# Seven modulation vectors on TensorE at the stage changes, the others on VectorE

## The chip, the cores and the metric

The kernel runs on one core of one Trainium2 chip. The metric is the device time of one execution in microseconds (us); the time before is the median of three runs. Everything shown of one execution comes from the hardware profiler. Engines are called PE (TensorE matmul), PEld (its weight load), DVE (VectorE), ACT (ScalarE), POOL (GpSimd) and SP (SyncE, which issues the transfers).

## The reference

Two networks follow one another on 256 tokens of width 1024, each two layers deep. Every layer is modulated: a vector of 6 x 1024 numbers is a product of the conditioning vector `c` and a 1024 x 6144 matrix, and its six parts shift, scale and gate the two halves of the layer.

```python
c_act = jax.nn.silu(c)
for l in range(DEPTH):
    mod = c_act @ ada_w[l] + ada_b[l]
    sh1, sc1, g1 = mod[:, None, 0:D], mod[:, None, D:2 * D], mod[:, None, 2 * D:3 * D]
    sh2, sc2, g2 = mod[:, None, 3 * D:4 * D], mod[:, None, 4 * D:5 * D], mod[:, None, 5 * D:6 * D]
    h = rmsnorm(x, norm1_g[l]) * (1.0 + sc1) + sh1
    x = x + g1 * token_mix(h, ...)
    h = rmsnorm(x, norm2_g[l]) * (1.0 + sc2) + sh2
    x = x + g2 * grouped_moe(h, ...)
```

The second network has the same frame with a gated linear recurrence (layer 0), a chunked attention (layer 1) and a 4096-wide MLP in each layer. With two more vectors for its shared keys and values there are 26 modulation vectors of 1024, numbered v = 0 to 25; `v = 6 * layer + part` with the four layers in order.

## The kernel before

The activations `xT` stay in SBUF, transposed, as 8 tiles of 128 x 256. All weights come from HBM once, as pieces of 128 x 2048 numbers (1 MB). A piece goes through a ring of 5 buffers (`raw`), is cut into a high and a low part (`parts_of`: ACT casts at L442, DVE subtracts at L443), and each product takes three matmuls of these parts (`mm3`, L453 to L455).

The stages follow one another: token mix, router and experts (MoE) for each layer of the first network, then recurrence, MLP, attention, MLP. Between two of them PE has to wait. The sum of squares of the new `xT` (`stats_add`) goes through DVE and POOL (`stats_close`, `power`), PE spreads it over the partitions (`rstd_x`, tile `ps_bc`), and `norm_mod` makes the next input `h_hi`, `h_lo` tile by tile on DVE and ACT. After the token mix it is the router (`route`) that PE waits for, twice: for the one-hot groups `oh` ahead of the matmuls into `ps_sl`, and for the gather matrix `both` ahead of `ps_xg`. At the end of each MoE stands a branch (`tc.If(big > 0)`, L1487) that every engine takes.

A modulation vector is 4 units of 1 MB. `ada_unit` computes a unit in one of two ways. On PE it is 8 matmuls into `adaps` (L331), 32 columns wide, four of them side by side; each shows as two records. The fourth unit is copied by ACT and folded by two further matmuls (`ada_flush`, tile `ps_mod`, L347). On DVE, for the vectors in the table `ON_DVE`, it is two fused multiply-and-sum instructions over 128 x 1024 (`ada_dve`, L305).

The units stand in one list (`pend`, L684). At numbered places of the program (`ada_site`, L364) the table `FILL` says how many units are taken from it, one where the table is silent. The program is written once; a scheduler then orders the instructions of every engine, and it may put matmuls of one unit between those of other work. `issue_after` holds an instruction behind a given one.

Of the kernel before, what the change touches and what calls it, by code (L numbers as in the profile page):

```python
# [53 lines left out]
ON_DVE = (2, 5, 6, 7, 8, 9, 12, 13, 14, 15, 19, 20, 24, 25)  # L54
# [128 lines left out]
def program(tc, A, out, dbg=None):  # L183
    nc = tc.nc
    from contextlib import ExitStack, nullcontext
    with ExitStack() as st:
# [129 lines left out]

        def ada_unit(u):
# [4 lines left out]
            raw = ring.tile([P, RING], F32, tag="raw", name="raw")  # L322
            nc.sync.dma_start(raw, A["ada"][u])
# [126 lines left out]

        def mm3(ps, a, b, start, stop):
# [1424 lines left out]
```

## Time and profile before

| | us |
|---|---|
| median of 3 runs (1825.03 to 1833.75) | 1825.52 |
| the profiled execution, its own time | 1829.82 |
| its span, first to last instruction | 1828.0 |

| engine | busy us | share of the span | instructions |
|---|---|---|---|
| PE | 1748.5 | 96% | 12430 |
| PEld | 1548.3 | 85% | 12430 |
| DVE | 1465.6 | 80% | 2514 |
| ACT | 1130.7 | 62% | 1758 |
| POOL | 37.4 | 2% | 40 |

Busy means that an instruction of the engine was in execution. Matmuls overlap and their ends are modelled, so a busy PE isn't PE at its peak. The transfers moved 485.62 MB, a mean of 266 GB/s. In the rows further down, times count from the start of the span, "x" is a count of records, PEclk is the granted TensorE clock (1.00 is 2.4 GHz, 0.50 is 1.2 GHz), and the square brackets at the end of a timeline row hold how long the engine had been idle and who released it.

### The profile page before, as it was taken

To read this page: it belongs to the slowest core of one execution; us is meant where nothing else is said; L and a number is where in the kernel's file an instruction comes from. 1 tells how busy PE (TensorE), PEld (TensorE's weight loads), DVE (VectorE), ACT (ScalarE), POOL (GpSimd) and SP (SyncE) were. 2 spreads that over 40 slices of the span, in tenths; PEclk is the share of its full clock that TensorE was granted. 3 is DMA by queue.
4 is the path that set the end of the run, shared out by engine and by line. 5 is a ranking of instruction groups with operands and counts; after the bars stand their busy time and mean duration, and the time that the engine had idled before them with its cause. 6 is when DMAs were issued, how large, how long until landed. Compare 5 with 4: busy or idle time off the path is not lost. (4 is left out here: it accounts for less than half of the span.)

```text
span 1828.0 us, 31671 instructions
## 1 busy us (share of the span) xinstructions
PE 1748.5 (96%) x12430; PEld 1548.3 (85%) x12430; DVE 1465.6 (80%) x2514; ACT 1130.7 (62%) x1758; POOL 37.4 (2%) x40
## 2 busy tenths in 40 slices
PE   7999998999999899998999999899999999999999
PEld 5877897888877897887888887798899988889999
DVE  4878897999998676888998999788898666667754
ACT  4754546877777556545877777578655446546642
POOL 0000000000000000000000000000000002100000
PEclk9999999999999899998999999899999999999999
DMA  9665797797998357688697899656687764456552
GB/s 354 234 248 213 278 358 278 287 348 278 350 346 343 137 191 265 233 323 343 253 343 301 328 354 354 236 202 251 221 322 284 272 250 146 173 191 256 204 193 84
DMA packets 71727, 485.62 MB, mean 266 GB/s; under 512 B 8720, under 2 KB 10896, under 8 KB 14352
## 3 DMA queue, kind: packets, MB, share of 16 engines
q1 hardware_dynamic: 70992, 483.21, 70.7%
q8 instruction: 101, 1.65, 0.4%
q14 instruction: 58, 0.48, 0.1%
q10 hardware_dynamic: 576, 0.27, 0.1%
HBM read 482.41 MB, written 1.05 MB: 264 GB/s over the span
## 5 line engine op out<-in xcount | busy, mean ns | idle before, releaser
L443 DVE TENSOR_TENSOR wlo<-raw,whi 128x1024 fp32r<-128x1024 f32 (+1 forms) x628 | 753.0, 1210 | 152.2 <-ACT whi L442 135.8
L442 ACT CAST whi<-raw 128x1024 fp32r<-128x1024 f32 (+1 forms) x628 | 649.7, 1041 | 282.8 <-PE ps_mm L454 164.6
L453 PE MATMUL ps_mm<-h_hi,whi 128*128 128x256 f32 x1168 | 329.7, 285 | 5.5 <-ACT h_hi L649 3.5
L454 PE MATMUL ps_mm<-h_lo,whi 128*128 128x256 f32 x1168 | 327.9, 282 | 0.7 <-DVE h_lo L650 0.7
L455 PE MATMUL ps_mm<-h_hi,wlo 128*128 128x256 f32 x1168 | 327.4, 282 | 1.0 <-DVE wlo L443 1.0
L453 PEld LDWEIGHTS ps_mm<-h_hi,whi 128*128 128x128 f32 x1168 | 222.0, 191 | 11.9 <-ACT h_hi L649 5.3
L454 PEld LDWEIGHTS ps_mm<-h_lo,whi 128*128 128x128 f32 x1168 | 222.6, 191 | 2.6 <-DVE h_lo L650 0.9
L455 PEld LDWEIGHTS ps_mm<-h_hi,wlo 128*128 128x128 f32 x1168 | 221.6, 190 | 3.6 <-DVE wlo L443 2.7
L454 PE MATMUL ps_e<-wlo,xg 128*128 128x512 f32 x512 | 202.5, 396 | 2.6 <-DVE wlo L443 2.3
L453 PE MATMUL ps_e<-whi,xg 128*128 128x512 f32 x512 | 202.7, 396 | 1.2 <-ACT whi L442 1.0
L455 PE MATMUL ps_e<-whi,xg 128*128 128x512 f32 x512 | 200.3, 391 | 0.0
L455 PE MATMUL ps_mm<-a_hi,wlo 128*128 128x256 f32 x512 | 142.2, 278 | 0.2 <-DVE wlo L443 0.2
L454 PE MATMUL ps_mm<-a_lo,whi 128*128 128x256 f32 x512 | 142.3, 278 | 0.0
L453 PE MATMUL ps_mm<-a_hi,whi 128*128 128x256 f32 x512 | 142.2, 278 | 0.0
L305 DVE SCALAR_TENSOR_TENSOR raw<-raw,cb 128x1024 f32<-128x1024 f32 x112 | 135.7, 1217 | 3.5 <-DMA raw<-in_ada_dram 3.4
L454 PEld LDWEIGHTS ps_e<-wlo,xg 128*128 128x128 f32 x512 | 96.2, 188 | 27.2 <-DVE wlo L443 8.5
L453 PEld LDWEIGHTS ps_e<-whi,xg 128*128 128x128 f32 x512 | 96.2, 188 | 20.9 <-ACT whi L442 1.8
L455 PEld LDWEIGHTS ps_e<-whi,xg 128*128 128x128 f32 x512 | 96.1, 188 | 18.5
L454 PE MATMUL py<-wlo,hT 128*128 128x512 f32 x256 | 101.0, 394 | 0.0
L455 PE MATMUL py<-whi,hT 128*128 128x512 f32 x256 | 99.8, 390 | 0.0
L453 PE MATMUL py<-whi,hT 128*128 128x512 f32 x256 | 99.5, 391 | 0.0
L455 PEld LDWEIGHTS ps_mm<-a_hi,wlo 128*128 128x128 f32 x512 | 96.0, 187 | 0.4 <-DVE wlo L443 0.4
(694 smaller groups left out, 3471.4 us busy)
## 6 DMA issues: line engine op xcount, KB each, us to landing
raw<-in_ada_dram SPq DMA_DIRECT2D x104, 1024.0 KB, 6.1
raw<-in_mw_dram SPq DMA_DIRECT2D x64, 1024.0 KB, 4.9
raw<-in_w_up_dram SPq DMA_DIRECT2D x56, 1024.0 KB, 5.0
raw<-in_w_down_dram SPq DMA_DIRECT2D x56, 1024.0 KB, 5.0
raw<-in_w_gate_dram SPq DMA_DIRECT2D x44, 1024.0 KB, 4.9
raw<-in_win_dram SPq DMA_DIRECT2D x34, 1024.0 KB, 5.2
more<-in_w_gate_dram SPq DMA_DIRECT2D x12, 1024.0 KB, 5.4
raw<-in_lwin_dram SPq DMA_DIRECT2D x11, 1024.0 KB, 7.4
```

Source lines behind the costliest of these rows:

```text
L305: nc.vector.scalar_tensor_tensor(w, w, 1.0, cb, op0=OP.mult, op1=OP.mult, accum_out=mod[:, m:m + 1])
L442: nc.scalar.copy(hi[:, :n], src)
L443: nc.vector.tensor_sub(lo[:, :n], src, hi[:, :n].bitcast(F32))
L453: nc.tensor.matmul(ps, ah, bh, start=start, stop=False)
L454: nc.tensor.matmul(ps, ah, bl, start=False, stop=False)
L455: nc.tensor.matmul(ps, al, bh, start=False, stop=stop)
```

## The change

Before, 12 vectors are computed on PE (0, 1, 3, 4, 10, 11, 16, 17, 18, 21, 22, 23) and 14 on DVE. After it, 9 are on PE and 17 on DVE. Of the nine, vectors 1 and 0 stay where they are, in the first 50 us. The other seven (5, 8, 11, 14, 17, 20, 23: the gates) leave the list and get places in the seven stage changes: `GAPS` says how many of the four units stand ahead of the last sum of squares or the router's sums, how many after it, and how many behind `ps_bc` (or behind `ps_sl`). `in_turn` ties the matmuls around them into that order, and their folding waits for the next `ada_flush`. At the end of a MoE their four loads are issued early (`EARLY_U`), and of the next stage's weights one piece is fetched ahead instead of three. `FILL` is new, and its default is no unit. In the core of the diff:

```diff
-ON_DVE = (2, 5, 6, 7, 8, 9, 12, 13, 14, 15, 19, 20, 24, 25)
+ON_DVE = (2, 3, 4, 6, 7, 9, 10, 12, 13, 15, 16, 18, 19, 21, 22, 24, 25)
+GAPS = {5: (0, 3, 1), 8: (0, 2, 2), 11: (0, 3, 1), 14: (0, 3, 1), 17: (1, 1, 2), 20: (1, 1, 2), 23: (1, 1, 2)}
...
+        def in_turn():
+            return tc.issue_after(PE_[0].ins) if PE_[0] else nullcontext()
+
+        def ada_load(u):
+            if u in EARLY_U:
+                return EARLY_U.pop(u)
+            raw = ring.tile([P, RING], F32, tag="raw", name="raw")
+            nc.sync.dma_start(raw, A["ada"][u])
+            return raw
...
-            ada_flush()
+            if u // 4 not in GAPS:
+                ada_flush()
...
+        def gap(v, i):
+            u = 4 * v + sum(GAPS[v][:i])
+            with in_turn():
+                for j in range(GAPS[v][i]):
+                    ada_unit(u + j)
...
-            ada_fill(FILL.get(i, n))
+            ada_fill(FILL.get(i, 0))
...
-        def stats_close(rt=None):
+        def stats_close(rt=None, v=None):
+            if v:
+                PE_[:] = LAST
+                gap(v, 0)
+                with in_turn():
+                    stats_late()
             stats_late()
...
-            for i in range(n):
-                nc.tensor.transpose(ps[:, i * P:(i + 1) * P], ST["rt"][:, i:i + 1].to_broadcast([P, P]), ident)
+            for i in (2, 3, 0, 1)[4 - n:]:
+                with in_turn():
+                    PE_[:] = [nc.tensor.transpose(ps[:, i * P:(i + 1) * P], ST["rt"][:, i:i + 1].to_broadcast([P, P]), ident)]
...
-        def norm_mod(a_col, b_col, rs=None, fill=0):
+        def norm_mod(a_col, b_col, rs=None, v=0):
             if rs is None:
                 rs = rstd_x()
-            ada_site(fill)
+            ada_site(0)
+            gap(v, 2)
...
-        pend += [4, 5, 6, 7, 0, 1, 2, 3] + list(range(8, 84)) + list(range(96, 104)) + list(range(84, 96))
+        pend += [4, 5, 6, 7, 0, 1, 2, 3] + [4 * v + i for v in ON_DVE[:-4] + (24, 25, 21, 22) for i in range(4)]
...
                 ada_site(TURN_1)
+                gap(5 + 6 * l, 1)
...
-                nc.tensor.matmul(pp[:, 0:4], lowb, oh[:, 0, :], start=True, stop=True)
+                with in_turn():
+                    nc.tensor.matmul(pp[:, 0:4], lowb, oh[:, 0, :], start=True, stop=True)
...
+                gap(5 + 6 * l, 2)
...
                             ready(nxt[:1])
+                            for u in range(32 + 24 * l, 36 + 24 * l):
+                                EARLY_U[u] = ada_load(u)
...
-                prefetch(nxt[1:])
+                prefetch(nxt[1:2])
+                gap(8 + 6 * l, 1)
+                PE_[0] = None
```

Line numbers of the changed kernel are 10 to 40 higher for the same code: L342 is its L331, L303 its L305.

**PE, router of layer 0.** `lowb` and `oneb` are constant matrices, `ps_ht` is the transposed input, `ps_sl` counts the tokens of each group. Before:

```order
L1212 MATMUL ps_ht<-c_ident,y 128x128
L583 MATMUL ps_ms<-c_wr,y 128x16
L1212 MATMUL ps_ht<-c_ident,y 128x128
L1254 LDWEIGHTS lowb
L1254 MATMUL ps_sl<-oh,lowb 128x4
L1255 LDWEIGHTS oneb
```

And now:

```order
L1241 MATMUL ps_ht<-c_ident,y 128x128
L605 MATMUL ps_ms<-c_wr,y 128x16
L1241 MATMUL ps_ht<-c_ident,y 128x128
L342 MATMUL adaps<-raw,crep 32x256 x24
L1285 LDWEIGHTS lowb
L1285 MATMUL ps_sl<-oh,lowb 128x4
L1286 LDWEIGHTS oneb
```

Three units of vector 5 have come between the last transposition and the group counts; the fourth stands behind the counts. Layer 1 has the same with vector 11.

**PE, end of the MoE of layer 0**, behind the branch (the row of `ps_ms` belongs to the path that isn't taken). Before:

```order
L583 MATMUL ps_ms<-one,sq 128x1 x2
L1487 UNCONDITIONAL_BRANCH x2
L632 MATMUL ps_bc<-c_ident,rx 128x128 x2
L453 MATMUL ps_mm<-h_hi,whi 128x256 x2
L454 MATMUL ps_mm<-h_lo,whi 128x256
L455 MATMUL ps_mm<-h_hi,wlo 128x256
```

And now:

```order
L605 MATMUL ps_ms<-one,sq 128x1 x2
L1524 UNCONDITIONAL_BRANCH x2
L342 MATMUL adaps<-raw,crep 32x256 x15
L660 MATMUL ps_bc<-c_ident,rx 128x128 x2
L342 MATMUL adaps<-raw,crep 32x256 x8
L475 MATMUL ps_mm<-h_hi,whi 128x256 x2
L476 MATMUL ps_mm<-h_lo,whi 128x256
L342 MATMUL adaps<-raw,crep 32x256 x8
L477 MATMUL ps_mm<-h_hi,wlo 128x256
```

One matmul of vector 8 stands ahead of the branch and 15 stand behind it, ahead of `ps_bc`. At the end of layer 1 it is 5 matmuls of vector 14 ahead of the branch and 19 behind it.

**DVE, heads of the token mix of layer 1** (`at` is the attention matrix of a head, `mk` its masked part). Before:

```order
L443 TENSOR_TENSOR wlo<-raw,whi 128x384
L972 TENSOR_TENSOR at_7832<-at_7832,mk 128x2x64
L972 TENSOR_TENSOR at_7832<-at_7832,mk 128x4x32
L972 TENSOR_TENSOR at_7832<-at_7832,mk 128x8x16
L972 TENSOR_TENSOR at_7832<-at_7832,mk 128x16x8
L972 TENSOR_TENSOR at_7832<-at_7832,mk 128x32x4
L972 TENSOR_TENSOR at_7832<-at_7832,mk 128x64x2
```

And now:

```order
L463 TENSOR_TENSOR wlo<-raw,whi 128x1024
L1001 TENSOR_TENSOR at_7837<-at_7837,mk 128x2x64
L303 SCALAR_TENSOR_TENSOR raw,mod<-raw,cb 128x1024
L1001 TENSOR_TENSOR at_7837<-at_7837,mk 128x4x32
L1039 TENSOR_TENSOR rt<-ps_rot,sn 128x256
L1001 TENSOR_TENSOR at_7837<-at_7837,mk 128x8x16
L1040 TENSOR_TENSOR qt<-qt,cs 128x256
```

Modulation instructions have come between a head's own. Between the scale `qsc` and the first output `ob_lo` of the other attention there are now 11 where there was none (layer 0: 9 where there were 4). The count of these instructions goes from 38 to 48 in the token mix of layer 1 and from 34 to 48 from the first MLP on; in layer 0 it stays 40.

## Rows read from the trace of the kernel before

**Rows 1.** Table by stretch, all work: length, PE, PEld, DVE, ACT, POOL busy, PEclk.
```profile
106.00:163.00 57.00, 54.73 (x422) 40.89 (x422) 43.49 (x165) 30.70 (x74) 4.36 (x5) 1.00 0.58 218
679.00:733.00 54.00, 53.13 (x442) 42.15 (x442) 38.70 (x123) 32.85 (x75) 3.29 (x4) 1.00 0.63 234
1166.00:1277.00 111.00, 107.41 (x933) 97.25 (x934) 93.34 (x173) 79.06 (x138) 0.00 (x0) 0.97 0.62 230
1317.00:1493.00 176.00, 175.26 (x1488) 174.05 (x1487) 136.87 (x210) 88.46 (x134) 0.00 (x0) 1.00 0.77 281
1518.00:1623.00 105.00, 101.84 (x866) 85.68 (x864) 69.59 (x181) 62.15 (x161) 14.07 (x13) 1.00 0.45 166
```

**Rows 2.** The same for tile `adaps` alone: length, PE, PEld, ACT busy, PEclk.
```profile
106.00:163.00 57.00, 13.27 (x128) 4.00 (x128) 0.74 (x2) 1.00 0.58 218
679.00:733.00 54.00, 10.82 (x128) 3.50 (x128) 0.75 (x2) 1.00 0.63 234
1166.00:1277.00 111.00, 13.60 (x160) 5.03 (x160) 0.73 (x2) 0.97 0.62 230
1518.00:1623.00 105.00, 10.13 (x112) 3.55 (x112) 0.38 (x1) 1.00 0.45 166
```

**Rows 3.** Groups of instructions: shapes, count, busy us, mean ns, idle before.
```profile
L305 DVE SCALAR_TENSOR_TENSOR raw<-raw,cb 128x1024 f32<-128x1024 f32 x112 | 135.7, 1217 | 3.5 <-DMA raw<-in_ada_dram 3.4
```

**Rows 4.** The chain that ended last, by line, 1166 to 1277 and 1518 to 1599.
```profile
by line: PE ps_mm L453 11.6%; PE ps_mm L454 10.8%; PE ps_mm L455 10.1%; DVE wlo L443 9.2%; PE adaps L331 7.9%; issue 6.8%; ACT whi L442 6.7%; DMA raw<-in_lwin_dram 5.3%; DMA raw<-in_band_dram 2.9%; ACT r L1616 2.6%; ACT r L1629 2.0%; ACT s_
by line: PE ps_mt L453 11.1%; PE ps_mt L454 9.7%; PE ps_mt L455 9.6%; PE ps_mm L453 9.2%; PE ps_mm L454 9.1%; PE ps_mm L455 8.0%; PE ps_ao L1180 5.5%; PE adaps L331 4.5%; PE ps_sc L1795 4.4%; POOL rk L549 3.9%; PE ps_pt L1172 3.1%; PE ps_hn
```

**Rows 5.** Timeline: a run of modulation records, at 2.4 and at 1.2 GHz.
```profile
1647.56 1.93 PE L331 MATMUL adaps<-raw,crep 128*32 128x256 f32 x30
1167.39 1.93 PE L331 MATMUL adaps<-raw,crep 128*32 128x256 f32 x16
```

**Rows 6.** Timeline of PE at the router of layer 0.
```profile
288.80 0.16 PE L1254 MATMUL ps_sl<-oh,lowb 128*128 128x4 bf16 x1 [3.38 <-DVE oh L1241]
291.01 0.55 PE L1316 MATMUL ps_xg<-both,ht_hi 128*128 128x256 f32 x1 [1.94 <-DVE both L1266]
```

**Rows 7.** The branch: its line on PE's queue (ns), then PE behind it.
```profile
L1487 PEldq COMPARE_BRANCH  x2: 3843/4712/5582, 594.3 to 1158.5; - x2
...
598.58 0.66 PE L632 MATMUL ps_bc<-c_ident,rx 128*128 128x128 f32 x2 [3.08 <-DVE gh L1130]
600.41 0.80 PE L453 MATMUL ps_mm<-h_hi,whi 128*128 128x256 f32 x2 [1.18 <-ACT h_hi L649]
...
1164.62 1.09 PE L632 MATMUL ps_bc<-c_ident,rx 128*128 128x128 f32 x4 [4.44 <-PEq L1487]
```

**Rows 8.** Timeline of PE: first product of the first MLP and of the attention.
```profile
1308.65 1.22 PE L453 MATMUL ps_mm<-h_hi,whi 128*128 128x256 f32 x4 [1.11 <-ACT h_hi L649]
1498.60 0.58 PE L453 MATMUL ps_mt<-whi,h_hi 128*128 128x256 f32 x1 [1.52 <-ACT h_hi L649]
```

**Rows 9.** Table by stretch at stage changes; after POOL: PEclk, DMA share, GB/s.
```profile
245.00:299.00 54.00, 45.98 (x373) 44.26 (x372) 46.51 (x101) 27.44 (x47) 0.70 (x1) 0.94 0.88 351
287.70:294.50 6.80, 3.76 (x21) 3.71 (x21) 5.96 (x17) 2.95 (x6) 0.00 (x0) 0.50 1.01 428
847.50:857.70 10.20, 5.03 (x29) 4.70 (x29) 7.64 (x24) 5.01 (x9) 0.70 (x1) 0.50 1.01 426
591.50:605.20 13.70, 9.45 (x41) 8.80 (x42) 7.06 (x19) 4.19 (x10) 0.70 (x1) 0.50 0.17 69
1154.70:1171.80 17.10, 11.34 (x57) 9.08 (x57) 8.87 (x25) 6.51 (x13) 1.01 (x1) 0.50 0.31 109
1308.30:1311.70 3.40, 3.05 (x14) 3.05 (x15) 3.40 (x10) 2.35 (x6) 0.00 (x0) 0.50 0.50 207
1496.00:1502.90 6.90, 4.99 (x22) 4.59 (x23) 5.38 (x14) 2.98 (x7) 0.34 (x1) 0.51 1.01 427
1643.00:1655.00 12.00, 11.54 (x125) 8.72 (x125) 8.87 (x22) 6.12 (x12) 0.70 (x1) 1.00 0.84 343
```

More of the change, by code (lines that the diff above doesn't have):

```diff
@@ L315, in ada_step @@
                 tiles.pop(0)()
+        EARLY_U = {}
+        PE_ = [None]
+        def in_turn():
[6 more added lines that the diff above has]
+            return raw
         def ada_unit(u):
@@ L321, in ada_unit @@
                 return ada_dve(u)
-            raw = ring.tile([P, RING], F32, tag="raw", name="raw")
-            nc.sync.dma_start(raw, A["ada"][u])
+            raw = ada_load(u)
             i, ps = 0 if u < 48 else 1, adaps[:, u // 4 % 2]
@@ L449, in parts_of @@
             return w
+        LAST = [None]
         def mm3(ps, a, b, start, stop):
@@ L673, in stats_late, with last_linear @@
                 stats_add(LATE_M.pop())
-        def last_linear(pcs, kt, x, gcol, fill=0, also=None):
+        def last_linear(pcs, kt, x, gcol, fill=0, also=None, v=None):
             stats_open(also=also)
             linear(pcs, kt, x, residual(gcol, True), fill)
-            stats_close()
-        pend += [4, 5, 6, 7, 0, 1, 2, 3] + list(range(8, 84)) + list(range(96, 104)) + list(range(84, 96))
+            stats_close(v=v)
+        pend += [4, 5, 6, 7, 0, 1, 2, 3] + [4 * v + i for v in ON_DVE[:-4] + (24, 25, 21, 22) for i in range(4)]
         with ExitStack() as es:
@@ L879, in token_mix @@
                     ada_site(HM)
-                    h = norm_mod(gain(at[f"n1_{l}"], M(0, l, 1)), M(0, l, 0), fill=NM)
+                    h = norm_mod(gain(at[f"n1_{l}"], M(0, l, 1)), M(0, l, 0), v=8)
                     linear(pc(0, 512), 8, h, ev_f, 0, True)
@@ L1299, in moe @@
                 ada_site(TURN_2)
-                ada_flush()
                 ready([(A["w_gate"][l * NE * 2], 0, 4, 0, 512)])
@@ L1376, in moe @@
                 back(0, 2)
+                ada_flush()
+                if two:
+                    c_columns(1)
                 U = {}
@@ L1501, in moe @@
                     stats_all(two, rt)
+                PE_[0] = None
         LAM = {}
@@ L1562, in recurrent @@
                 nc.vector.tensor_mul(ga, ga, at["fin"])
-                h = norm_mod(ga, M(1, 0, 0), rs=rs[:, T:], fill=NL)
+                h = norm_mod(ga, M(1, 0, 0), rs=rs[:, T:], v=14)
                 xc = (lr.tile([P, 11, T], F32R, name="xc_hi"), lr.tile([P, 11, T], F32R, name="xc_lo"))
@@ L1692, in recurrent @@
                         residual(M(1, 0, 2), True)(c + i, accs[c + i])
-                stats_close()
+                stats_close(v=17)
         def mlp(l):
@@ L1702, in mlp @@
                 ada_site((HP, HQ)[l])
-                h = norm_mod(gain(at[f"m2_{l}"], M(1, l, 4)), M(1, l, 3), fill=(NP, NQ)[l])
+                gap(17 + 6 * l, 1)
+                h = norm_mod(gain(at[f"m2_{l}"], M(1, l, 4)), M(1, l, 3), v=17 + 6 * l)
                 a = (mp.tile([P, 32, T], F32R, name="a_hi"), mp.tile([P, 32, T], F32R, name="a_lo"))
@@ L1715, in mlp @@
                 if l + 1 < DEPTH:
-                    last_linear(*out_, M(1, l, 5), FM)
+                    last_linear(*out_, M(1, l, 5), FM, v=20)
                 else:
@@ L1732, in chunk_attn @@
                 ada_site(HA)
+                gap(20, 1)
                 rs = ap_.tile([P, T], F32, name="rs")
                 nc.scalar.copy(rs, rstd_x())
-                hk = norm_mod(gain(at["kvn"], mod[:, o + 8:o + 16]), mod[:, o:o + 8], rs=rs, fill=NA)
+                hk = norm_mod(gain(at["kvn"], mod[:, o + 8:o + 16]), mod[:, o:o + 8], rs=rs, v=20)
                 h = (ap_.tile([P, 8, T], F32R, name="hq_hi"), ap_.tile([P, 8, T], F32R, name="hq_lo"))
@@ L1842, in chunk_attn @@
                 linear(wo[1:], 8, oo, out_, FA)
-                stats_close()
+                stats_close(v=23)
         for l in range(DEPTH):
```

18 lines of the change are left out of this document (9 added, 9 removed), and 10 rows, old and new, of the table FILL.

## The prediction

> **What bounds the kernel now.** I read the table by stretch first. PE is busy for 54.73 of 57 us in the heads of layer 0, for 53.13 of 54 in those of layer 1, for 107.41 of 111 in the recurrence and for 175.26 of 176 in the first MLP, always ahead of DVE [rows 1]. So PE sets the pace inside the stages. The same table for the tile `adaps` alone says how much of that is modulation: 13.27, 10.82, 13.60 and 10.13 us in four stretches, 47.82 us in all, made by 528 records, that is 33 of the 48 units [rows 2]. This is what could leave PE's path. But DVE is not far behind in the same stretches: 43.49 of 57, 38.70 of 54, 93.34 of 111, 69.59 of 105 [rows 1], and the price of a vector on DVE is high: 8 instructions of 1217 ns [rows 3], 9.7 us, three vectors more are 29 us. So the question in each stretch is how far it can shrink before DVE ends it.
>
> **The change, part by part.** The sum is made against the profiled execution, 1829.8 us; the median of the runs lies 4.3 lower, at 1825.5.
>
> *Heads of layer 0.* PE loses 13.27 us. DVE gets 5 modulation instructions more between the same two landmarks, 5 x 1.217 = 6.1, so 43.49 + 6.1 = 49.6 us of DVE in a stretch of 57: it can't shrink by more than 7.4 us, and by nothing if the heads' own chain sets it. I take 6, near the upper end, since PE stood still for only 57 - 54.73 = 2.3 us.
>
> *Heads of layer 1.* PE loses 10.82 us, DVE gets 11 more, 13.4 us: 38.70 + 13.4 = 52.1 of 54. At most 1.9 us; I take 1.5.
>
> *Recurrence.* PE loses 13.60 us and DVE gets nothing here. The chain that ended last says what of it was on the path: 7.9% of 111 us, 8.8 us [rows 4]. The same row has 5.3%, 5.9 us, for the landing of a recurrence weight; its piece shares the five ring buffers with modulation loads that are now gone, and I take 2 of them. Together 10.8; the ends are 8.8 and 13.6 + 5.9 = 19.5.
>
> *Attention.* PE loses 10.13 us. In the first 81 us of the stretch the chain has 4.5%, 3.6 us, for it [rows 4]; the last 24 us have no such row, and of what lies there, 10.13 less what the first part holds, about 4.9, I take half: 6.0. Ends 3.6 and 10.1.
>
> Sum of what goes: 24.3 us, between 12 and 39.
>
> *What comes into the waits.* The price of a unit: 30 records, 15 matmuls, took 1.93 us at 2.4 GHz and 16 records the same at 1.2 GHz [rows 5], so a unit of 8 matmuls is 1.03 or 1.93 us.
>
> At the router PE waits 3.38 us for `oh` and 1.94 us for `both` [rows 6]. Three units (3.1 us) and one (1.0) fit in. Cost 0, in both layers; a cover of 0.3 and 0.9 us is left, so it costs something as soon as a load is late.
>
> At the end of the MoE it is different. PE's branch takes 3.84 us in layer 0 and 5.58 in layer 1 on its own queue, and the waits ahead of `ps_bc`, 3.08 and 4.44 us, are this branch [rows 7]: the row that releases it is PE's sequencer, or DVE released by it. The order puts 15 matmuls of vector 8 (19 of vector 14) behind the branch and ahead of `ps_bc`, so they don't fill the wait, they prolong it: 1.93 us (2.4) at full clock, 3.6 (4.6) at half. Queued behind them are `ps_bc`, then DVE's and ACT's chain of `h_hi`, `h_lo`, and all of the next stage. The unit after `ps_bc` meets a wait of 1.18 us [rows 7] and overhangs by 0 or 0.75; layer 0 has another unit among the products, 1.03 or 1.93. Ends 3.0 and 6.3 for layer 0, 2.4 and 5.4 for layer 1. The granted clock there is 0.50 from 591.5 to 605.2 and from 1154.7 to 1171.8 [rows 9], so I stay nearer to the upper ends: 5 + 4 = 9. Whoever took the 3.08 and 4.44 us for idle time to be filled would write 0 here, and get 9 us less. The Trainium skill, Runtime: NRT & Kernel Launch, section on instruction fetch mechanics, speaks for the reading above: a taken branch whose target is not in the window already fetched makes the engine fetch the target before it goes on, so by that page no work behind the branch can cover it. The two durations of 3.84 and 5.58 us agree.
>
> Before the two MLPs and the attention, the first unit has the wait for the last squares, the second the wait for POOL, and two units (2.06 us) stand behind `ps_bc`, where PE waits 1.11 and 1.52 us [rows 8]: overhang 0.95 + 0.5, I take 1.5, and 0 where the tiles of `h` come slowly enough to take it up. The change from attention to the second MLP has its four units there already, and stays.
>
> *The clock.* In that last change, with four units in its waits, PEclk is 1.00 and PE is busy for 11.54 of 12 us; in the two like it with 3 us and more of waiting it falls to 0.50 for 3.40 and 6.90 us [rows 9]. If these stay up, half of PE's busy time there is saved, 1.5 and up to 2.5; DVE, busy for 5.38 of 6.90, allows about 1.5 in the second. At the routers DVE is busy for 5.96 of 6.80 us and 7.64 of 10.20, so 0.5 each. I take -4; ends 0 and, with the rest of the stretches, -18.8 (below).
>
> *DVE from the first MLP on.* 14 instructions more, 17 us, beside 136.87 of 176 us in the first MLP alone. They fit; PE has 0.74 us of idle to show there, so little can be late now. I take +2, with 0 and 17 as the ends.
>
> *Loads.* The same 104 units are loaded. Four of the five ring buffers are held by modulation at each change, and the next weights come later; I take 0 and price it as a rival.
>
> Sum: -24.3 + 9 + 1.5 - 4 + 2 = -15.8. 1829.8 - 15.8 = 1814.0 in a profiled execution, 1825.5 - 15.8 = 1809.7 as a median: **1810 us**. With its own bounds, some 1800 to 1820.
>
> **The rivals.**
>
> *The clock stays up everywhere.* In six stretches of 58.1 us together PE runs at 0.50 and is busy for 3.76 + 5.03 + 9.45 + 11.34 + 3.05 + 4.99 = 37.6 us [rows 9]. If the new work lifts all of it, half is saved, 18.8 instead of 4, and the two MoE ends cost their lower ends, 5.4 instead of 9: -24.3 + 5.4 + 1.5 - 18.8 + 2 = -34.2, 1791 us. For it: the filled change at 1643 never fell. Against it: at the MoE ends the clock is down before the change begins (from 591.5, with `ps_bc` at 598.58), and DVE is busy for most of the router stretches. The Trainium skill, TensorE: Matmul & The Clock Gate, Part 1, has the rule behind it: idleness throttles the array to half rate and sustained work releases it. 0.20.
>
> *DVE becomes the bound.* The heads and the attention don't shrink because DVE's new instructions stand between a head's own, on the chain of each head; only the recurrence gains: -10.8 + 9 + 1.5 - 4 + 2 = -2.3, 1823 us. For it: 52.1 of 54 us in layer 1. Against it: in layer 0 and in the attention DVE has room. 0.20.
>
> *The gaps' loads come late: slower.* From 245 to 299 us the transfers already run at 351 GB/s with a DMA share of 0.88 [rows 9]. Four pieces of 1.05 MB more are 4 x 3.0 = 12 us of transfer; the idle share gives back 0.12 x 54 = 6.5. So the last piece is 5.5 us late, 12 at worst, in each layer, and the group counts stand behind these matmuls on PE, the whole MoE behind them. At the MoE ends three of the next stage's pieces come after the gap's four, up to 9 us late each time. All of it is 11 to 42 us; in the middle, 28, it gives 1825.5 - 15.8 + 28 = 1838. It decides from 16 us on (no gain left) and makes the kernel slower beyond 25. Against it: fewer modulation loads come earlier in the token mix (32 units before the first MoE instead of 36), and the heads run at a DMA share of 0.58 and 0.63 only [rows 1]. 0.12.
>
> **How the numbers follow.** Forecast 0.48, clock 0.20, DVE 0.20, late loads 0.12. A difference of 0.5%, 9.1 us, is about the least that a measurement of this kernel can tell from none. The forecast's own range lies below 1816.4 for five sixths (0.40), the clock case wholly (0.20), the DVE case at its upper end (0.03): faster 0.63. Slower, above 1834.6: most of the late loads and DVE's end of 17 us, 0.12. Within: 0.25. The range goes from just under the clock case, 1788, to 1832, past the DVE case and short of the late loads' middle.
>
> **What would show it.** Right: no `adaps` records between the products of the heads, the recurrence and the attention; these stretches shorter by about 6, 1.5, 11 and 6 us; the two waits at the router under 1 us, with `ps_sl` no later; `ps_bc` at the MoE ends 2 to 5 us later behind the branch; PEclk 1.00 before the first MLP and the attention. Wrong: `adaps` waiting for its load at the router; DVE without idle time in the heads and PE waiting for it; PEclk still 0.50 in the filled changes; the first MLP longer by more than 2 us.

## The result, and the profile after

| | before | change |
|---|---|---|
| median, same session, us | 1825.54 (4 runs, 1825.03 to 1833.75) | 1849.45 (4 runs, 1847.29 to 1855.03) |
| a later session, us | 1832.70 | 1845.92 (1843.41 to 1851.54) |
| profiled execution, its time and span, us | 1829.82, 1828.0 | 1850.52, 1848.7 |

The ratio is 1.0112 with a 95% interval of 1.0085 to 1.0140, in the later session 1.0084 (1.0052 to 1.0115). 1810 us was predicted, 1788 to 1832: the kernel became slower by about 1%, not faster.

Seven stretches from landmark to landmark, in the table by stretch (length, PE, PEld, DVE, ACT, POOL busy, PEclk, DMA share, GB/s): token mix of layer 0, MoE 0, token mix of layer 1, MoE 1, recurrence, attention, last MLP. A token mix runs from its first product to the group counts `ps_sl`, a MoE from the first `ps_xg` to the next `ps_bc`, recurrence and attention from their first product to the next `ps_bc`. The kernel before:

```profile
22.20:288.80 266.60, 254.22 (x2080) 224.25 (x2081) 215.94 (x545) 148.10 (x295) 6.60 (x7) 0.99 0.73 274
291.00:598.60 307.60, 300.47 (x1401) 246.81 (x1401) 279.12 (x314) 232.30 (x261) 0.70 (x1) 0.98 0.83 315
600.40:851.90 251.50, 239.84 (x1944) 217.73 (x1945) 198.19 (x446) 139.17 (x274) 7.28 (x7) 0.98 0.68 250
854.10:1164.60 310.50, 301.25 (x1400) 247.16 (x1401) 281.55 (x321) 232.74 (x262) 1.01 (x1) 0.98 0.84 315
1166.90:1307.10 140.20, 134.89 (x1186) 123.31 (x1186) 118.77 (x210) 97.26 (x163) 0.70 (x1) 0.98 0.64 235
1498.60:1647.20 148.60, 142.30 (x1187) 123.03 (x1187) 98.56 (x241) 84.00 (x201) 19.54 (x17) 0.99 0.48 179
1649.40:1824.30 174.90, 174.88 (x1543) 174.67 (x1540) 107.17 (x146) 87.98 (x133) 0.00 (x0) 1.00 0.51 183
```

And the changed kernel:

```profile
24.80:288.10 263.30, 247.14 (x1993) 221.59 (x1994) 214.66 (x543) 146.63 (x291) 6.49 (x7) 0.96 0.67 249
289.40:601.90 312.50, 306.03 (x1436) 248.90 (x1436) 277.80 (x313) 231.51 (x261) 0.70 (x1) 0.98 0.85 319
603.50:862.40 258.90, 239.51 (x1876) 218.05 (x1876) 209.91 (x470) 139.84 (x274) 6.76 (x7) 0.96 0.69 253
863.80:1175.70 311.90, 305.85 (x1453) 248.15 (x1453) 278.50 (x319) 231.50 (x261) 1.01 (x1) 0.98 0.84 320
1177.50:1314.60 137.10, 125.76 (x1023) 121.43 (x1023) 118.87 (x209) 99.05 (x164) 0.70 (x1) 0.95 0.52 186
1506.50:1661.10 154.60, 139.72 (x1073) 122.88 (x1069) 115.18 (x274) 85.28 (x201) 19.62 (x17) 0.94 0.54 197
1663.30:1844.90 181.60, 181.60 (x1544) 181.42 (x1540) 107.43 (x146) 87.85 (x133) 0.00 (x0) 1.00 0.51 178
```

The differences are -3.3, +4.9, +7.4, +1.4, -3.1, +6.0 and +6.7 us; the first product of all stands 2.6 us later (22.2, 24.8), and the other stage changes and the first MLP make -2.0. To rounding that is the 20.7 us between the spans.

Look at the four streams (token mixes, recurrence, attention): in them PE's records of `adaps` were busy for 17.55 + 10.82 + 15.54 + 12.89 = 56.8 us before and are for 8.73 + 5.22 + 2.14 + 2.19 = 18.3 after. So 38.5 us of matmuls left. But length less PE busy, PE's idle time, went from 12.4 + 11.7 + 5.3 + 6.3 = 35.7 to 16.2 + 19.4 + 11.3 + 14.9 = 61.8: 26.1 us of the room came back as waiting. And PEclk fell in each of the four: length times (1 - PEclk) rises by 7.9 + 5.3 + 4.1 + 7.8 = 25 us. That is the most that the clock can have cost, since PE was idle in part of it. The other 12.4 us of the room, and the 7.0 us by which the four stages together grew, are 19.4 us that PE was busy for longer with the same work; the clock is enough to account for them.

The waits themselves, in the view of waits of PE. Token mix of layer 1, recurrence, attention of the change (waited for: us, times, longest):

```profile
PE ps_ot L1023 <- DVE o L1019: 4.1, 2, 3.2
PE ps_rot L1037 <- ACT qt L1079: 2.5, 1, 2.5
...
PE ps_bd L475 <- DVE mod L368: 3.8, 1, 3.8
PE ps_bd L475 <- ACT r L1654: 3.4, 2, 2.9
...
PE ps_pt L1201 <- DVE p L1196: 4.1, 2, 3.3
PE ps_kt L1801 <- DVE rk L570: 3.4, 1, 3.4
```

Before, `ps_ot` waited for 1.3 us in all, `ps_bd` for 2.7, `ps_pt` for 1.7 and `ps_kt` for 2.5, with none above 1.9. The 3.8 us ahead of `ps_bd` are not simply cover that has gone: as their releaser the profile has the addition that ends the late folding of vector 14, which the change itself put there and which DVE comes to only behind the recurrence's own instructions:

```profile
1217.70 0.15 DVE L368 TENSOR_TENSOR mod<-ps_mod,c_adab 128x8 f32<-128x8 f32 x1
1217.92 0.55 PE L475 MATMUL ps_bd<-xc_hi,whi 128*128 128x256 f32 x1 [3.80 <-DVE mod L368]
```

E13 below tests it. Behind the new waits the clock drops. The table by stretch around three of them, in token mix 1 and at the start and end of the attention:

```profile
727.00:740.00 13.00, 7.77 (x30) 5.49 (x30) 11.34 (x36) 5.25 (x15) 1.67 (x1) 0.61 0.60 210
1515.00:1525.00 10.00, 7.32 (x39) 6.68 (x40) 4.85 (x8) 4.22 (x7) 1.85 (x2) 0.66 0.80 318
1631.00:1641.00 10.00, 7.92 (x41) 5.99 (x42) 3.74 (x12) 4.62 (x13) 0.00 (x0) 0.66 0.02 10
```

At the branch [rows 7] the timeline of the change shows the sequence that was forecast: the branch, then 30 records (15 matmuls) at half rate, then `ps_bc`, at 601.91 us instead of 598.58:

```profile
598.34 3.63 PE L342 MATMUL adaps<-raw,crep 128*32 128x256 f32 x30 [1.62 <-PEq L1524]
601.91 0.32 PE L660 MATMUL ps_bc<-c_ident,rx 128*128 128x128 f32 x1
```

At the router [rows 6] both waits are gone, but the clock is still 0.50 from 284.4 to 287.8, so the three units take 4.48 us, a little more than the wait that they fill:

```profile
283.65 4.48 PE L342 MATMUL adaps<-raw,crep 128*32 128x256 f32 x48
288.07 0.18 PE L1285 MATMUL ps_sl<-oh,lowb 128*128 128x4 bf16 x1
```

At the start of the program the change has an effect that I had overlooked. `rstd_x` ties its transpositions behind the last matmul of `ada_unit`, and here that is the last of vectors 1 and 0:

```profile
14.93 4.80 PE L342 MATMUL adaps<-raw,crep 128*32 128x256 f32 x54
19.66 0.43 PE L660 MATMUL ps_bc<-c_ident,rx 128*128 128x128 f32 x2
...
24.75 0.60 PE L864 MATMUL ps_f<-y_hi,whi 128*128 128x256 f32 x2 [3.92 <-ACT y_hi L832]
```

Before, this `ps_bc` came at 15.91 and the first product at 22.16.

The last MLP has the same 1536 products, the same PEclk of 1.00 and no idle time, and still takes 6.7 us longer: 181.60 us of PE for 1544 records against 174.88 for 1543, 117.6 ns against 113.3 from one product to the next.

### The profile page after: what moved, and what is told of

Same layout as the page of the kernel before. It is cut to its first block, busy times and chain, and to the rows that moved or that the text cites. A ratio compares the mean times of both kernels' runs of the same rounds, so it can differ in the third digit from the quotient of the medians.

```text
span 1848.7 us, 31295 instructions
## 1 busy us (share of the span) xinstructions
PE 1752.4 (95%) x12226; PEld 1556.3 (84%) x12226; DVE 1487.4 (80%) x2562; ACT 1130.2 (61%) x1755; POOL 36.9 (2%) x40
## 3 DMA queue, kind: packets, MB, share of 16 engines
q8 instruction: 99, 1.62, 0.3%
## 5 line engine op out<-in xcount | busy, mean ns | idle before, releaser
L303 DVE SCALAR_TENSOR_TENSOR raw<-raw,cb 128x1024 f32<-128x1024 f32 x136 | 164.5, 1215 | 2.8 <-DMA raw<-in_ada_dram 2.7
L475 PEld LDWEIGHTS ps_mm<-a_hi,whi 128*128 128x128 f32 x512 | 96.3, 188 | 0.0
```

What stands on the lines that cost most here:

```text
L303: nc.vector.scalar_tensor_tensor(w, w, 1.0, cb, op0=OP.mult, op1=OP.mult, accum_out=mod[:, m:m + 1])
L475: nc.tensor.matmul(ps, ah, bh, start=start, stop=False)
```

## The experiments

Three theories. **A, lost cover:** the modulation in the streams stood in waits of the stages' own chains and held the clock; without it the waits lie open and TensorE slows down. **B, VectorE's queue:** the 1.2 us instructions that VectorE got delay a stage's small ones. **C, the prediction's:** a unit on TensorE costs its length.

Two cautions hold for all that follows. A stage's length comes from one profiled execution of each kernel. In six profiles with the token mix 0 of the change this stage took 262.1 to 269.0 us; in six with its token mix 1, or nearly, 257.1 to 265.9; in five with its attention, 153.1 to 154.6. The kernel before is steadier: the stages that E10 shares with it repeat within 2.4 us. And the scheduler orders a stage anew when something is left out of it or added. In E10's token mix 1, 185 of TensorE's 1808 other records and 54 of VectorE's 367 stand in another sequence than in the kernel before. In E7 it is 10 of TensorE's 985 in the recurrence and 30 of 1033 in the attention. What the other order alone does was not measured.

**Each engine alone (E1, E2, E3).** Vectors 3, 4, 10, 16, 18, 21, 22 at the change's places on TensorE, on no engine, or on VectorE with filler on TensorE. E1 (and E8 and E12) also has E14's tie and a second buffer for `ada_s`.

```diff
E1  -ON_DVE = (2, 3, 4, 6, 7, 9, 10, 12, 13, 15, 16, 18, 19, 21, 22, 24, 25)
    +ON_DVE = (2, 6, 7, 9, 12, 13, 15, 19, 24, 25)
     ...
E2  +            if v in (3, 4, 10, 16, 18, 21, 22):
    +                if u % 4 == 3:
    +                    tiles.append(lambda: nc.vector.tensor_copy(mod[:, 8 * v:8 * v + 8], adab[:, 8 * v:8 * v + 8]))
    +                return
E3  +            if u // 4 in (3, 4, 10, 16, 18, 21, 22):
    +                for r in range(2):
    +                    for j in range(4):
    +                        nc.tensor.matmul(adaps[32 * j:32 * j + 32, u // 4 % 2], crep[:, 4 * r + j, :],
    +                                         cb[:, j * T:(j + 1) * T], start=r == 0, stop=r == 1, tile_position=(0, 32 * j))
```

E1: 

> The seven vectors 3, 4, 10, 16, 18, 21, 22 go back from VectorE to TensorE, each unit at the same place of the list and of the program (3, 4 in the token mix of layer 0; 10, 16 in that of layer 1; 18 in the first MLP; 21, 22 in the attention). The units in the stage changes stay, and the recurrence has no unit either way, so it is a control. Against the changed kernel (1849.5 us; token mix of layer 1 252 us from first to last product, attention 152, recurrence 132). Theory A, lost cover: in these streams the modulation matmuls stood in waits that a stage's own chain makes, and kept TensorE's clock at full rate; with them back the token mix of layer 1 takes about 246 us and the attention 146, half-clock time there falls from 23.6 and 23.9 us of the two stages to under 10 each, and the whole is about 1837. Theory B, VectorE's queue: the 1.2 us instructions that VectorE got stand ahead of a head's own; it gains as much here, since they are gone too, so this run doesn't tell A from B. Theory C, the one on record: matmuls on TensorE's path cost their length, 28 units of 1.03 us: about 1878.

E2: 

> The changed kernel without the computation of vectors 3, 4, 10, 16, 18, 21, 22 on any engine: their loads stay, the 56 fused instructions on VectorE are left out (of each vector only the bias is copied). Theory A: the waits are the stages' own, so they stay, and the clock falls as before: token mix of layer 1 about 250 us, attention about 151, whole 1845 to 1849. Theory B: with VectorE's instructions gone the waits go: token mix of layer 1 about 240, attention about 142, whole about 1827. Theory C says the same as B.

E3: 

> The changed kernel, and at the place of each unit of vectors 3, 4, 10, 16, 18, 21, 22 TensorE also does 8 matmuls of a unit's size on constants that are in SBUF, into adaps, which nobody reads; VectorE does its instructions as in the change. 224 matmuls more, nothing less. Theory A: no slower, since they stand in waits and hold the clock: token mix of layer 1 about 247, attention about 147, whole about 1838 to 1845. Theory B: the waits stay where VectorE is late and the matmuls come on top in part: 1849 to 1865. Theory C: 28 x 1.03 = 29 us more, 1878.

Medians 1860.61, 1826.94 and 1856.31 us beside 1828.74 for the kernel before: ratios 1.0149 (1.0095 to 1.0204), 0.9985 (0.9963 to 1.0008), 1.0150 (1.0111 to 1.0189). Token mix 0, token mix 1 and attention of E2, then token mix 0 and 1 of E1 and of E3, by stretch:

```profile
25.60:281.00 255.40, 243.53 (x1992) 220.54 (x1993) 197.74 (x509) 146.32 (x291) 5.64 (x7) 0.98 0.69 254
595.60:847.40 251.80, 234.65 (x1878) 215.77 (x1879) 193.45 (x435) 139.59 (x274) 6.81 (x7) 0.97 0.69 257
1487.10:1638.40 151.30, 137.15 (x1072) 122.82 (x1068) 99.01 (x240) 84.46 (x201) 17.10 (x17) 0.94 0.55 202
...
23.70:288.80 265.10, 255.02 (x2128) 224.38 (x2128) 200.15 (x512) 147.96 (x295) 5.50 (x7) 0.99 0.64 242
608.40:869.50 261.10, 248.99 (x2014) 224.59 (x2011) 192.74 (x436) 139.94 (x275) 7.41 (x7) 0.96 0.67 250
...
25.80:288.00 262.20, 251.95 (x2120) 221.39 (x2121) 213.66 (x542) 146.62 (x291) 7.45 (x7) 0.99 0.67 247
605.00:875.50 270.50, 256.12 (x2010) 228.77 (x2007) 210.38 (x470) 140.42 (x274) 6.76 (x7) 0.94 0.66 242
```

Leaving 16 instructions off VectorE in each of these stages makes them shorter by 7.9, 7.1 and 3.3 us than in the change's first profile: 0.5, 0.4 and 0.2 us for an instruction of 1.2. Against the shortest of the change's profiles it is 6.7, 5.3 and 1.8. So B has a part, which A denied. E1 against E2 puts TensorE's price on the same units, at the same places: 265.1 - 255.4 = 9.7 us for 8 units in token mix 0, 261.1 - 251.8 = 9.3 in token mix 1, 156.2 - 151.3 = 4.9 in the attention; by the medians the 28 units cost 33.7 us. A missed there too: at the change's places a unit isn't free in a token mix. **The exchange itself wins next to nothing: in the token mixes a unit costs about 1.2 us on TensorE and 0.9 to 1.0 on VectorE, each against a kernel that does it on neither.** The two prices don't add up. E3 has VectorE's instructions and TensorE's filler in one stage: token mix 1 got longer by them (270.5), but token mix 0, with 8 units of filler on top, took 262.2 us, no more than the change without them, and the attention got shorter, 154.6 to 152.1, with PEclk at 0.98 instead of 0.94. And E2 leaves A its place: token mix 1 has no unit in its stream and 32 instructions on VectorE where the kernel before had 8 units and 38, and is no shorter than before.

**The units ahead of the branch (E4).**

```diff
-... 8: (0, 2, 2), ... 14: (0, 3, 1), ...
+... 8: (2, 0, 2), ... 14: (2, 0, 2), ...
...
-                rt = stats_close()
+                rt = stats_close(v=8 + 6 * l)
-                gap(8 + 6 * l, 1)
```

> The changed kernel with the two (layer 1: three, now two) units of vectors 8 and 14 at the ends of the MoE tied in ahead of the last sum of squares, as the MLPs have them, so that they stand ahead of the branch; two units stay behind ps_bc. If matmuls behind the branch are all cost: ps_bc comes after the branch as it did before the change, 3.3 and 2 us earlier than in the change, and the whole is about 1844. If the units only move the wait (the last sum is late by as much): ps_bc unchanged, 1849. If they also hold the clock ahead of the branch: up to 4 us more, 1840.

The MoE took 313.5 and 313.4 us to `ps_bc`, not less than 312.5 and 311.9 (median 1854.86, ratio 1.0144, 1.0107 to 1.0182). In layer 0:

```profile
598.60 1.01 PE L605 MATMUL ps_ms<-one,sq 128*128 128x1 f32 x4
602.83 0.66 PE L660 MATMUL ps_bc<-c_ident,rx 128*128 128x128 f32 x2 [3.22 <-PEq L1523]
```

Behind the branch PE waits for 3.22 us again (1.62 in the change), and the last sum of squares, which stood at 594.75, comes 3.9 us later: at the end of a MoE the units cost about the same on either side of the branch.

**Token mix 1 bare, and nothing at the MoE ends (E5).** As E2, for more vectors, and without the units and loads of 8 and 14.

```diff
-            if v in (3, 4, 10, 16, 18, 21, 22):
+            if v in (3, 4, 9, 10, 12, 13, 15, 16, 18, 21, 22):
...
+            if v in (8, 14):
+                if i == 1:
+                    nc.vector.tensor_copy(mod[:, 8 * v:8 * v + 8], adab[:, 8 * v:8 * v + 8])
+                return
             u = 4 * v + sum(GAPS[v][:i])
...
-                            for u in range(32 + 24 * l, 36 + 24 * l):
-                                EARLY_U[u] = ada_load(u)
```

> The changed kernel with the modulation of vectors 3, 4, 9, 10, 12, 13, 15, 16, 18, 21, 22 left out of VectorE (loads stay), so that the token mix of layer 1 has no modulation instruction on VectorE at all; and with the eight units of vectors 8 and 14 at the ends of the two MoE left out with their loads. Lengths from landmark to landmark, before / change / the run that left seven vectors out: token mix of layer 1, first product to group counts, 251.5 / 258.9 / 251.7 us with 38 / 48 / 32 such instructions; MoE, first product of the gathering to ps_bc, 307.6 / 312.5 / 310.8 and 310.5 / 311.9 / 311.9. Theory B (each instruction on VectorE in a head delays the head): 32 instructions of about 0.45 us less, token mix of layer 1 about 237 us. Theory A (the waits are the heads' own and only the cover is lost): 247 to 252. Ends of the MoE: if the units behind the branch are all cost, ps_bc comes at 307.6 and 310.5 again, else at 311 and 312.

Median 1809.84, ratio 0.9916 (0.9891 to 0.9942). MoE 0, token mix 1 and MoE 1:

```profile
281.10:589.90 308.80, 300.76 (x1404) 246.47 (x1405) 279.07 (x315) 232.04 (x261) 0.70 (x1) 0.98 0.85 323
591.70:834.40 242.70, 231.75 (x1856) 216.13 (x1857) 158.00 (x363) 138.08 (x272) 5.61 (x7) 0.98 0.69 256
836.60:1144.40 307.80, 300.36 (x1405) 245.86 (x1405) 279.62 (x318) 232.39 (x262) 1.01 (x1) 0.99 0.84 321
```

Against E2 the 32 instructions were worth 9.1 us, 0.28 each, not the 14 of B, but more than the 0 to 5 of A: without modulation in its heads the stage takes 243. The units at the ends cost 3.7 and 4.1 us, near the prediction's 5 and 4.

**Filler at the places of the kernel before (E6).** 10 units in the recurrence, 8 in the attention, by the numbers of the places; the loops are E3's.

```diff
             ada_fill(FILL.get(i, 0))
+            for _ in range({98: 1, 99: 2, 102: 1, 103: 1, 105: 2, 107: 3, 133: 2, 136: 1, 139: 1, 141: 1, 142: 3, 143: 0}.get(i, 0)):
+                for r in range(2):
...
```

> The changed kernel, and in the recurrence (10) and the attention (8) filler of a unit's 8 matmuls on constants, at about the places of the program where the kernel before had its units there (those at the very edges moved inward). Recurrence, first product to ps_bc, before / change: 140.2 / 137.1 us; attention, first product to ps_bc: 148.6 / 154.6. Theory A (they stood in waits and held the clock): recurrence not above 138, attention 149 to 152, although 18 units of 1.03 us come on top. Theory C (length on TensorE's path): recurrence 147, attention 163. If only half of them stands in waits: 142 and 158.

Recurrence and attention:

```profile
1188.60:1324.50 135.90, 132.87 (x1182) 121.92 (x1182) 119.24 (x209) 99.00 (x164) 0.70 (x1) 0.99 0.52 188
1517.00:1669.00 152.00, 142.47 (x1201) 121.86 (x1197) 115.07 (x274) 85.04 (x201) 21.52 (x17) 0.99 0.54 200
```

18 units more, and neither stage is longer (137.1 and 154.6 in the change): idle time falls from 11.3 to 3.0 and from 14.9 to 9.5 us, PEclk rises from 0.95 and 0.94 to 0.99. That is A, and C is out by 11 us in each. That the recurrence got shorter isn't shown: without filler it took 134.3 to 138.1 us in ten profiles. The whole was 1843.64 (ratio 1.0095, 1.0060 to 1.0131).

**The kernel before without its stream units (E7).** The clean test of the term that I had subtracted.

```diff
+            if u // 4 in (3, 4, 10, 11, 16, 17, 18, 21, 22):
+                ada_flush()
+                if u % 4 == 3:
+                    v = u // 4
+                    tiles.append(lambda: nc.vector.tensor_copy(mod[:, 8 * v:8 * v + 8], adab[:, 8 * v:8 * v + 8]))
+                return
```

> The kernel before with the matmuls of vectors 3, 4, 10, 11, 16, 17, 18, 21, 22 left out (36 units; loads stay, of each vector only the bias is copied), nothing else changed: what these units cost in the kernel before, stage by stage. The prediction's terms: token mix of layer 0 shorter by 6 to 8 us (8 units), of layer 1 by 4 to 8 (8 units), recurrence by 8.8 to 13.6 (10 units), attention by 3.6 to 10 (8 units), whole about 1800. Theory A: the recurrence shorter by 3, the attention longer by 2 to 3, half-clock time in both up by 5 to 11; whole about 1815.

Median 1823.54 (ten runs, 1821.39 to 1824.35), ratio 0.9966 (0.9944 to 0.9987): 36 units, 37 us of matmuls at 1.03, were worth some 4 to 6 us. Token mix 0, token mix 1, recurrence, attention:

```profile
23.30:281.10 257.80, 241.77 (x1945) 220.25 (x1946) 214.91 (x544) 146.98 (x293) 6.60 (x7) 0.98 0.75 282
592.60:852.00 259.40, 237.53 (x1808) 220.47 (x1809) 199.75 (x448) 138.22 (x272) 5.54 (x7) 0.95 0.66 247
1165.40:1301.00 135.60, 122.70 (x987) 119.84 (x987) 118.01 (x207) 96.02 (x160) 0.70 (x1) 0.95 0.64 244
1493.30:1641.90 148.60, 138.13 (x1097) 121.97 (x1097) 99.09 (x240) 84.68 (x201) 18.68 (x17) 0.96 0.52 186
```

-8.8, **+7.9**, -4.6 and 0.0 us. In token mix 0 C is right. In the attention the units were free (82 records of them stood in this stretch, 6.2 us). In the recurrence 12 units, 15.5 us of records, were worth 4.6. Token mix 1, in another order, got longer with less work in it.

**A version between the two (E8).** The kernel before's list of units and places (`PLAN`), with vectors 5, 11, 17, 20, 23 alone in the changes, 8 and 14 on VectorE, and three pieces fetched ahead.

```diff
-GAPS = {5: (0, 3, 1), 8: (0, 2, 2), 11: (0, 3, 1), 14: (0, 3, 1), 17: (1, 1, 2), 20: (1, 1, 2), 23: (1, 1, 2)}
+GAPS = {5: (0, 3, 1), 11: (0, 3, 1), 17: (1, 1, 2), 20: (1, 1, 2), 23: (1, 1, 2)}
-ON_DVE = (2, 3, 4, 6, 7, 9, 10, 12, 13, 15, 16, 18, 19, 21, 22, 24, 25)
+ON_DVE = (2, 6, 7, 8, 9, 12, 13, 14, 15, 19, 24, 25)
...
-            ada_fill(FILL.get(i, 0))
+            for u in PLAN.get(i, ()):
+                ada_unit(u)
```

> A version between the two: the kernel before with its table of places, and only the vectors 5 and 11 (at the routers), 17, 20 and 23 (ahead of MLPs and attention) in the stage changes, tied in as in the change; nothing at the ends of the MoE, vectors 8 and 14 on VectorE as before; 3, 4, 10, 16, 18, 21, 22 stay on TensorE in the streams where they were. Against the kernel before 16 instructions leave VectorE and 8 units leave TensorE's streams. By the prices of the runs so far (a unit in a token mix about 1 us on TensorE, an instruction on VectorE about 0.45 us, units in the changes nothing): token mix of layer 0 -3 to -4, of layer 1 -2 to -4, recurrence 0 to -2, first MLP -2, changes -1: about 10 us faster than before. If cover and clock decide (theory A), the recurrence and the token mix of layer 1 lose what they gain: no change.

A miss: 1834.47 us, ratio 1.0040 (1.0023 to 1.0058). The recurrence gave 5.4 us, but four units of vector 18 had moved to the start of the first MLP, which became 195.5 us long (187.7), the attention took 153.0 (148.6), and token mix 1, from which four units had gone to the router, 252.2 (251.5).

**Token mix 1 again, from both sides, and the change again (E9 to E11).** E9 puts 8 units of filler at the places of vectors 10 and 11; E10 is E7 for these two alone; E11 is the change.

```diff
E9   +            for _ in range({64: 1, 65: 3, 66: 1, 69: 1, 70: 2}.get(i, 0)):
E10  +            if u // 4 in (10, 11):
```

> The changed kernel, and in the token mix of layer 1 filler of 8 units (8 matmuls each, on constants) at the places of the program where the kernel before had its vectors 10 and 11. Token mix of layer 1, first product to group counts, so far: before 251.5 us, change 258.9 (other kernels with the same program there 263.6 and 265.6). Theory A (at those places they stand in waits and hold the clock): 250 to 256 us and half-clock time below 12, although 8.2 us of matmuls come on top. Theory B and C: 267 us or more.

> The kernel before with only the 8 units of vectors 10 and 11 left out (loads stay). Theory A: token mix of layer 1 258 to 262 us instead of 251.5, half-clock time up from 6 to 15 or more, the whole 4 to 8 us slower than before. Theory C: token mix of layer 1 243 to 247 us and the whole 4 to 8 us faster.

> The changed kernel as it is, profiled again, for the spread of its stages. If the length of the last MLP (181.6 us in the first profile, at 117.7 ns from product to product; 174.9 and 113.3 ns before) is drawn anew in each execution: 175 or 181; if it belongs to the program: 181.6 again. Token mix of layer 1 259 to 266 us.

Token mix 1 of E9, of E10, and token mix 1 and last MLP of E11:

```profile
605.70:868.00 262.30, 249.56 (x2009) 221.07 (x2006) 210.39 (x470) 140.12 (x274) 7.66 (x7) 0.97 0.69 251
```

```profile
600.50:857.60 257.10, 238.12 (x1809) 221.47 (x1810) 199.88 (x447) 138.28 (x272) 5.53 (x7) 0.94 0.67 249
```

```profile
603.40:860.50 257.10, 236.94 (x1877) 216.66 (x1878) 209.26 (x469) 139.43 (x274) 6.76 (x7) 0.97 0.69 255
1663.00:1837.80 174.80, 174.80 (x1544) 174.63 (x1540) 107.14 (x146) 87.91 (x133) 0.00 (x0) 1.00 0.53 185
```

E10 comes out as A said: 8 units less, the stage 5.6 us longer (11.7 us of idle time become 19.0), the whole slower, ratio 1.0028 (1.0005 to 1.0050). But the other order of this stage is a rival for it that no run parts from lost cover; E7 has the same order. E9, whose order is nearly the change's, is neither A's nor C's: filler cut the idle time from 20.2 us to 12.7, and the stage took 262.3, inside the 257.1 to 265.9 that it takes without filler. So the 8 units cost nothing that can be told there, but they don't bring 251.5 back. How lost cover, VectorE's 48 instructions and the order divide what this stage lost stays open. E11's last MLP has 174.80 us: the 6.7 us of the first profile aren't the change's.

**Two places only (E12).** From E8, with 5 and 17 alone in the changes (11 and 23 back in their old places, 20 on VectorE), and vector 18 in the places that 17 leaves.

```diff
-GAPS = {5: (0, 3, 1), 11: (0, 3, 1), 17: (1, 1, 2), 20: (1, 1, 2), 23: (1, 1, 2)}
+GAPS = {5: (0, 3, 1), 17: (1, 1, 2)}
-PLAN = { ... 111: [72, 73, 74, 75], ...
+PLAN = { ... 103: [72], 105: [73, 74], 107: [75], ...
...
```

> The kernel before with its table of places, and only vector 5 (from VectorE, at the router of layer 0) and vector 17 (from the recurrence, ahead of the first MLP) in the stage changes; the units of vector 18 that stood in the first MLP move into the places that 17 leaves in the recurrence. Prices from the runs: token mix of layer 0 -1 to -4 us (8 instructions fewer on VectorE), recurrence -3 to -5, first MLP 0 to -2 (two units fewer on TensorE, none behind the change). 0.2 to 0.5% faster than before. If lost cover decides here too: no difference.

1827.74 us beside 1832.70: ratio **0.9980 (0.9965 to 0.9995)**, faster than both kernels, if by little. Token mix 0 took 263.9 us (266.6), the recurrence 137.9 (140.2), the first MLP 185.7 (187.7).

**Late weights, and the tie at the start (E13, E14).**

```diff
E13  +            if v in (8, 14, 20):
     ...
     +                return
     -                            for u in range(32 + 24 * l, 36 + 24 * l):
     -                                EARLY_U[u] = ada_load(u)
     -                prefetch(nxt[1:2])
     +                prefetch(nxt[1:])
E14  +                    if u // 4 in GAPS:
     +                        PE_[:] = [q]
```

> The changed kernel with the units of vectors 8, 14 and 20 in the stage changes left out together with their loads, and three pieces of the next stage's weights fetched ahead at the end of a MoE again, as before the change. In the change the attention's second piece of key and value weights lands 10.6 us after its issue, among modulation pieces, and TensorE waits 3.43 us ahead of ps_kt; in the recurrence it waits 3.80 us ahead of ps_bd. If the late weights make these waits (nothing else to do for TensorE): the 3.43 us fall to about 1 as in the kernel before, the attention from 154 (first product to ps_bc) to about 150; the recurrence from 137 to 133. If only the missing filler makes them: both waits stay within 0.3 us, attention 153, recurrence 137. The ends of the MoE 4 us shorter each, as in the run that left 8 and 14 out.

> The changed kernel, but only matmuls of the seven vectors in the stage changes set the instruction that later ones are tied behind. In the change the first ps_bc of the program comes behind all 54 records of vectors 1 and 0 (19.66 us, 15.91 before), and the first product of the token mix at 24.75 us, 22.16 before. Expected if the tie is the cause: ps_bc at 16, first product at 22 to 22.6, 2 to 3 us less in all; else 24.7 again.

First the change's attention, in the view of transfers (size, median us from issue to landing) and the timeline:

```profile
raw<-in_kvw_dram SPq DMA_DIRECT2D x2, 1024.0 KB, 10.6
```

```profile
1516.28 0.41 PE L1801 MATMUL ps_kt<-c_ident,kn 128*128 128x128 f32 x2 [3.44 <-DVE rk L570]
```

Then E13's:

```profile
raw<-in_kvw_dram SPq DMA_DIRECT2D x3, 1024.0 KB, 4.8
```

```profile
1527.14 0.41 PE L1803 MATMUL ps_kt<-c_ident,kn 128*128 128x128 f32 x2 [0.95 <-DVE kn L1798]
```

With the weights there in 4.8 us (4.7 before the change) TensorE has products to do, the wait shrinks to 0.95 us and the attention to 149.2 (154.6). The recurrence doesn't care (138.1, idle 11.7 us). Vector 14 isn't folded there now and the wait for it is gone, but others have taken its place; with filler, in E6, they were gone. The ends of the MoE are shorter by 4.7 and 4.6 us, as expected. The whole gained little, since the two token mixes, almost unchanged in their program, took 269.0 and 265.9 us in this execution. In E14 `ps_bc` stands at 15.71 and the first product at 22.39: the tie was the cause of the late start. Medians 1843.45 (ratio 1.0072, 1.0048 to 1.0096) and 1844.98 (1.0063, 1.0042 to 1.0084).

## Why the prediction was wrong

| term | predicted | measured |
|---|---|---|
| token mix 0 | -6 | -3.3 |
| token mix 1 | -1.5 | +7.4, +5.6 in the second profile |
| recurrence | -10.8 | -3.1 |
| attention | -6 | +6.0, +4.9 |
| MoE ends | +9 | +6.3; the units alone 3.7 + 4.1 |
| loads | 0 | 4 to 5 of the attention's |
| other stage changes: overhang, clock | +1.5 - 4 | -1.8 |
| DVE, first MLP | +2 | -0.2 |
| start | not seen | +2.6 |
| last MLP | not seen | +6.7, -0.1 in the second profile |

**The step that failed** is "so PE sets the pace inside the stages", and with it the sum of what goes, 24.3 us "between 12 and 39". I read a busy share of 96 to 98% in the four streams [rows 1] as a path, and subtracted what stood on it. But part of the busy time was the modulation itself, standing in waits: E7 takes the units out of the kernel before, and the four stages give -8.8, +7.9, -4.6 and 0.0. By the prediction's way of reckoning, with VectorE left as it was, they had to give -6 to -8, -4 to -8, -8.8 to -13.6 and -3.6 to -10. Token mix 0 about fits, the other three don't, and the recurrence and the attention miss with TensorE's other work in nearly the same order. The lower bounds came from the chain that ended last [rows 4]; a row there says that an instruction stood on the path, not that the path is shorter without it, since the next wait takes its place. So 8.8 and 3.6 were no lower bounds, and a loss of this size should have been inside the range.

**The clock had the wrong sign in the streams.** I priced it only at the stage changes, and there it mostly did what was forecast: before the first MLP and the attention it stayed at full rate (1.00 from 1314.6 to 1318.0 and from 1504.3 to 1508.5), and at the MoE ends it stayed down (0.61 from 595.7 to 603.5). At the routers it stayed at 0.50 for most of the first three units. So the rival in which it stays up everywhere (0.20) failed too. That the modulation also held it up inside the stages (PEclk 1.00, 1.00, 0.97 and, in the attention, 1.00) [rows 1] I didn't price. Where E6 gave the recurrence and the attention their filler back, PEclk went from 0.95 and 0.94 to 0.99, and 18 units more made neither stage longer.

**The rival "DVE becomes the bound"** (0.20) was half right: its instructions in the streams cost 0.2 to 0.5 us each (E2, E5). As a rival it was priced as no gain in the heads; it is a loss in token mix 1, beside the lost cover.

**The rival "loads come late"** (0.12) came true where it had no price: in the attention, by 4 to 5 us (E13). At its own places it failed: at the routers no modulation record waited for a load, and behind the second MoE three pieces fetched ahead instead of one left the recurrence as it was (E13).

**Right:** the branch. Its waits are no room, and the units behind it cost 3.7 and 4.1 us. That they cost as much ahead of it (E4) I had not said. Also right: no `adaps` among the products, both router waits under 1 us, the first MLP no longer. The -3.3 us of token mix 0 is less than the 6 forecast, and in other profiles of nearly the same program it lies between -4.5 and +2.4.

## What to carry to other kernels

A busy engine isn't a path: before counting the removal of filler as a gain, leave it out of the old kernel alone, see what the stage does, and look whether the scheduler kept the order of the rest. Filler that stands in waits costs little and holds TensorE's clock, so taking it away can give much less than its length, here nothing in the attention and 4.6 us of 15.5 in the recurrence. When work changes engines, price it by the difference between doing it there and not doing it at all, at the same place; in the token mixes it was about a microsecond a unit on either engine, and the two prices didn't add up where both engines had the work.

## What was not expected of the hardware

Long runs of products go at one of two paces, at a PEclk of 1.00 and without idle time: 113.3 ns (174.88 us for 1543 records) or 117.6 ns (181.60 for 1544). Two executions of the same program, the change and E11, had one each; E1 and E8 had the slow one (181.5 and 181.6 us), and three others (E6, E9, E12) took 178.2 us for the last MLP, and changed pace half way. What sets the pace isn't shown. It is worth 6.7 us in the last MLP alone, and is part of the 3 to 19 us between the runs of one kernel.

How long TensorE stays at half rate after the same waits also differs from execution to execution. Token mix 1 is almost the same program in the change, E4, E6, E11, E13 and E14, with 18 to 20 us idle in each; it took 258.9, 265.6, 263.5, 257.1, 265.9 and 263.6 us, longest where PEclk was lowest (0.93 in E4 and E13, 0.97 in E11). Where the clock hardly falls the stage is steady: the kernel before had 251.5 us, and E12, with the same program there, 251.0. So the +7.4 us of the first profile is one draw between some 6 and 14.
